# Second projection's operands prepared in two parts on VectorE, last norm factors stored by halves, second weight block rounded between decays

## The chip, the cores and the metric

The kernel runs on one core of one Trainium2 chip. The core has a matrix engine (TensorE, PE in the profile; its weight loads are PEld), VectorE (DVE), ScalarE (ACT), GpSimd (POOL) and SyncE (SP), which here only issues transfers. Each engine works through its own instructions in order and waits on semaphores for the others. Transfers between the chip's main memory (DRAM) and on-chip memory (SBUF) are issued by SP and by ScalarE. Matrix products gather in PSUM, which has eight banks of 128 x 512 values.

The metric is the device time of one execution in microseconds (us). The kernel before took 1428.77, 1432.49 and 1429.33 us in three runs, a median of 1429.33.

## The reference

One layer of a hybrid decoder on 1024 tokens of width 1024, in f32. The input is normed and modulated by a conditioning vector, projected once to all branches (`proj = h @ w_in`), and two branches are computed and merged:

```python
y_a = spatial_gating(gelu(gm_u), gelu(gm_v), ...) * silu(gm_z)
xbc = silu(causal_depthwise_conv(xbc, conv_w, conv_b))
xs, bm, cm = split(xbc, ...)                      # 2048, 8 x 128, 8 x 128
y_b = ssd_scan(xh, dt, a, bm, cm) + xh * d_skip   # 8 groups, chunks of 128 tokens
yz = (y_b * silu(ssm_z)).reshape(b, s, 8, 256)
y_b = rms_norm(yz, ssm_norm_w)                    # over the 256 channels of each group
merged = sigmoid(g_a) * (y_a @ w_proj_a) + sigmoid(g_b) * (y_b @ w_proj_b)
out = x + gate * (merged @ w_out)                 # then a final rms_norm over the width
```

`y_b` has 2048 channels, so `w_proj_b` is 2048 x 1024; `w_proj_a` and `w_out` are 1024 x 1024.

## The kernel before

Every large product is made of three products of 128 x 512 tiles: each operand is split into a high part (rounded by ScalarE, a cast) and a low part (the value less the high part, a subtraction on VectorE), and high x high, high x low and low x high are added in one PSUM bank.

The kernel runs in stages. First come the norm of the input and the input projection, each block of it as a scheme of seven half-size products p1 to p7 in place of eight. Then the scan: eight groups of 256 channels, each in four steps of 256 tokens (`front`, `back`, and `prep`, `decay` for the steps to come). Between the scan's steps TensorE is filled with the first projection, `y_a @ w_proj_a` (`proj_a`, a generator from which `draw(n)` takes n steps; PSUM tiles `pma`, result `tha`, stored to `mt_d`). Its weights come in eight blocks: `wa_load` loads one (`wa`), `wa_high` rounds it on ScalarE (`wah`), `wa_low` makes the low part on VectorE (`wal`). `decay_rows` and `decay_exps` make the scan's decay factors with exponentials on ScalarE (tiles `ea`, `dcy`) and a mask on GpSimd between them.

When a group's scan is through for half of the tokens (q is 0 or 1), `post` leaves its output `yz` in DRAM (`yb_d`) and, with a delay counted in slots of the program, squares it on ScalarE (`squares`), sums the squares over channels with TensorE (`post2`, bank `pq`) and reads the sums on VectorE (`post2b`, tile `ssq`). GpSimd raises them to the power -1/2, and `post3` turns them with a TensorE transpose into rows, copies those on VectorE (`cwt` for even groups, `tri` for odd ones) and stores them from ScalarE to `rs_d`. For groups 6 and 7 post3 is called in the second projection, into banks of p2 (`yp`), after the third and fourth unit of p1.

The second projection, `y_b @ w_proj_b`, follows, again by seven products, in the order p1, p2, p5, p3, p6, p7, p4. Each has eight k steps, so there are 56 units, of 12 matmuls of 128 x 512 each (`multiply`, L1548). A unit needs `loads(u)` on SP: the scan's output (`yn`), the norm factors of its group spread over all partitions (`rb`, one for two units, from `rs_d`), and the weights, which are raw for p1 and p2 (`p1r`, `p2r`, to be split) and split beforehand in DRAM for the others (`wb_d`). Then `operands(u)`: VectorE norms `yn` (`y_norm`), for some products forms a sum or difference of blocks, ScalarE rounds it (`bh`), VectorE makes the low part (`bl`), and for p1 and p2 ScalarE and VectorE split the weights in the same way (`p1a`, `p2a`). The tiles `bh` and `bl` have four places each, `rb` three, the weights nine.

The order is written out by hand in this stage: every instruction of VectorE, ScalarE and GpSimd is kept in program order. After each `multiply(u)` come `loads(u + 6)` and `operands(u + 4)` (`ahead`). After the last unit of a product `emptied_banks` frees its banks before `ahead`: ScalarE copies them (p1, p5, p3), or VectorE adds them to sums (`c<-c,yp` for p2, `p<-p,x` for p6 and p7). p2, p5 and p3 use four banks (`yp`), p1, p6, p7 and p4 the other four (`x`); a product that starts anew, as p5, waits until its bank is read. `merged` then multiplies a block by its gate and adds the other branch (tiles `tg`, `ma`, with the split `mmh`, `mml`), in odd units from p3 on. The output projection (`po`) and the final norm end the kernel.

Transfers complete on eight semaphores, which SP's and ScalarE's transfers take in turn, so that an issue waits for the transfer eight before it.

Of the kernel before, what the change touches and what calls it, by code (L numbers as in the profile page):

```python
# [35 lines left out]
def hybrid_kernel(  # L36
# [55 lines left out]
    def tp(dst, src, idn):  # L92
        pin(PE.transpose(dst, src, idn))  # L93
# [409 lines left out]
    def later(delay, f, *a):  # L503
        tasks.append((slot[0] + delay, f, a))
# [455 lines left out]
    class Group:  # L960
# [158 lines left out]
        def post(self, q):  # L1119

            g = self.g
            yz = self.yz[q]

            def leave():
                for j in range(2):
                    store(yb_d[2 * g + j][:, q * 512 : (q + 1) * 512], yz[:, j])

            if g < NG - 2 or q == 0:
                later(3, leave)
                later(9, self.squares, yz, [yz[:, j] for j in range(2)])  # L1130
                later(17, self.post2, q, yz[:, 0])
            else:
                later(1, leave)
                sq = [turn(r, f"sq{g}", F32) for r in ((y1_r, ym_r) if g < NG - 1 else (war_r[0], war_r[0]))]
                later(1, self.squares, yz, sq, pin)
                later(9, self.post2, q, sq[0])

        def squares(self, yz, sq, keep=lambda i: i):
# [11 lines left out]
        def post2b(self, q, pq):  # L1150
            g = self.g
            V.tensor_scalar(ssq[:, g * NCH + q * 4 : g * NCH + q * 4 + 4], pq[:, 0:4], 1.0 / 256, EPS,
                            op0=ALU.mult, op1=ALU.add)
            release(f"pq{g}_{q}")
            if q == 1:
                c8 = slice(g * NCH, (g + 1) * NCH)
                G.tensor_tensor(ssq[:, c8], ssq[:, c8], nhalf, op=ALU.pow)
                if g < NG - 2:
                    later(8, self.post3)

        def post3(self, at_once=False):

            g = self.g
            pr = rows_bank[0](f"pr{g}")
            tp(pr[0:NCH, 0:P], ssq[:, g * NCH : (g + 1) * NCH], ident)
            row = (cwt, tri)[g % 2][0:NCH, :]
            V.tensor_copy(row, pr[0:NCH, 0:P])
            release(f"pr{g}")
            to = rs_d[g].rearrange("o (c p) -> (o c) p", p=P)
            if at_once:  # L1170
                store(to, row)
            else:
                later(1, store, to, row)
# [171 lines left out]
    def proj_a():  # L1345

        for dd in range(KT):
# [8 lines left out]
            for k in range(KT):  # L1356
                wh, wl = was[dd][k // 4]
                yh, yl = yas[k]
                ks = slice(k % 4 * P, (k % 4 + 1) * P)
                for n, (lw, r) in enumerate(((wh, yh), (wh, yl), (wl, yh))):  # L1360
                    for h in range(2):
                        mm(pms[h], lw[:, ks], r[h], k + n == 0, k == KT - 1 and n == 2)
                    yield
                if k == 1 and dd + 1 < KT:
                    wa_high(dd + 1)
                if k == 3 and dd + 1 < KT:
                    wa_low(dd + 1)
            for h in range(2):
                V.scalar_tensor_tensor(ths[h], ths[h], 1.0, pms[h], op0=ALU.add, op1=ALU.mult)
# [10 lines left out]
    tha_r, ea_r, y1_r, ym_r = (ring(c) for c in (4, 3, 2, 2))  # L1380
    st_tag = room.pop(0)
    st_home = take("st_home", st_tag, F32)
    fetch(4)
    wa_load(1)
    fetch(5)
    while tasks:
# [5 lines left out]
    free.extend(BANKS)  # L1392
    for k in (6, 7):
        ya_operand(k)
    decays(4)
    fill = proj_a()

    left = [3 * KT * KT]
# [106 lines left out]
            n = k if nm == "p1" else KT + k  # L1505
            load(raw, w_proj_b[n * P : (n + 1) * P, 0:512])

    def operands(u):

        nm, k = units[u]  # L1510
        if nm in fresh:
            n, h = fresh[nm]
            y_norm(n + k, h)
        b11, b12 = yt[k, 0], yt.get((k, 1))
        b21, b22 = yt.get((KT + k, 0)), yt.get((KT + k, 1))
        t = {"p1": b11, "p2": b21, "p5": b12, "p3": b22, "p6": b12, "p7": b11, "p4": b21}[nm]
# [12 lines left out]
        if nm not in WB:  # L1529
            a, raw = aops[u], raws.pop(u)  # L1530
            keep(A.copy(a[:, 0], raw))
            keep(V.tensor_sub(a[:, 1], raw, f32(a[:, 0])))
        if nm == "p6":
            V.tensor_sub(b21, b21, b12)
# [83 lines left out]
    ya_free()  # L1618
    for tags in (war_r[0][0][:2], wah_r[0][0][2:], wal_r[0][0][2:], y1_r[0], ym_r[0], tha_r[0]):
# [44 lines left out]
    for u, (nm, k) in enumerate(units):  # L1664
# [153 lines left out]
```

## Time and profile before

| | us |
|---|---|
| median of three runs | 1429.33 |
| the profiled execution | 1429.86 |
| its span, first to last instruction | 1428.1 |
| TensorE busy | 1392.1 |
| VectorE busy | 1035.0 |
| ScalarE busy | 780.3 |
| GpSimd busy | 206.0 |
| second projection, from its first matmul to its last | 1161.0 to 1331.95 |

The mean granted clock of TensorE is 0.995 of full speed. The profile names an instruction by engine, line, operation and tiles: `p2bl<-yn,p2bh` writes the low part of a p2 operand from the normed output and its high part. Much of VectorE's and ScalarE's work passes through a helper and has its line, L56, so it is told apart by its tiles. A bracket at a row's end is the idle time of the engine just before it, and what ended that. "issue" as a releaser says that the profile shows nothing that the engine waited for. Busy time of a long row of matmuls runs a little over the space between their starts, since one matmul begins before the one ahead has ended.

### The profile page before, as it was taken

How to read it: one execution, taken by the hardware profiler on the slowest of the kernel's cores; microseconds unless marked ns; L12 is line 12 of the kernel's file. 1: busy time of each engine (PE TensorE's matmuls, PEld its weight loads, DVE VectorE, ACT ScalarE, POOL GpSimd, SP SyncE). 2: the span in 40 equal slices, each digit the busy share in tenths (PEclk: the TensorE clock that was granted, in tenths of full speed). 3: DMA queues.
4: the chain of work that ended last, by engine and by line, in shares of the span. 5: the costliest groups of instructions: out<-in, count | busy, mean ns of one | idle time of the engine just before them, and what ended most of it. 6: DMA issues, size and time to landing. Idle time of an engine off the chain costs nothing.

```text
span 1428.1 us, 20481 instructions
## 1 busy us (share of the span) xinstructions
PE 1392.1 (97%) x7087; PEld 1152.1 (81%) x7087; DVE 1035.0 (72%) x1827; ACT 780.3 (55%) x1438; POOL 206.0 (14%) x190
## 2 busy tenths in 40 slices
PE   8999999999999999999999999999999998999997
PEld 6688888888888888888887788878888876877886
DVE  5686676777667888788877885668878757677743
ACT  6664576566656665555665455667767523223401
POOL 0000000000000000000010100037878820000000
PEclk9999999999999999999999999999999999999999
DMA  9552333333332677586686764799779478976531
GB/s 281 147 162 89 119 118 104 104 103 113 109 110 90 206 225 225 176 261 208 184 252 195 221 189 141 243 325 307 276 260 324 163 261 300 332 245 215 186 118 74
DMA packets 260524, 277.08 MB, mean 194 GB/s; under 512 B 13596, under 2 KB 210628, under 8 KB 260420
## 3 DMA queue, kind: packets, MB, share of 16 engines
q1 hardware_dynamic: 179396, 195.37, 43.5%
q10 hardware_dynamic: 81024, 80.40, 16.2%
q8 instruction: 56, 0.92, 0.3%
q14 instruction: 48, 0.39, 0.1%
HBM read 191.40 MB, written 84.31 MB: 193 GB/s over the span
## 4 chain that ended last, share of the span: by engine, by line
PE 68%; DMA 11%; DVE 9%; ACT 5%; issue 3%; POOL 3%; SPq 1%; ACTq 0%; POOLq 0%; DVEq 0%
PE xuz L585 6%; PE xcb L585 6%; PE xx L585 5%; PE xz L585 5%; PE po L90 4%; PE xg L585 4%; PE yuz L585 3%; PE xv L585 3%; PE ycb L585 3%; PE yz L585 2%; PE yg L585 2%; PE yx L585 2%; PE pma L90 2%; PE yp L1548 2%; PE yv L585 2%
## 5 line engine op out<-in xcount | busy, mean ns | idle before, releaser
L796 POOL TENSOR_TENSOR wog<-wog,gb 128x1024 f32<-128x1024 f32 x8 | 22.4, 2796 | 725.8 <-DMA wbr<-in_w_proj_b_dram 569.4
L56 ACT ACTIVATE dcy<-dcy,nacs 128x128 f32<-128x128 f32 x256 | 78.4, 389 | 34.3 <-POOL dcy L56 18.2
L56 POOL TENSOR_SCALAR_AFFINE_SELECT dcy<-dcy 128x1024 f32<-128x1024 f32 x32 | 37.3, 1166 | 105.5 <-ACT ea L56 105.3
L908 ACT ACTIVATE ac<-ac 128x1024 f32<-128x1024 f32 x32 | 34.0, 1061 | 19.7 <-DVE ac L906 19.6
L90 PE MATMUL pma<-yh,wah 128*128 128x512 f32 x128 | 43.2, 419 | 0.1
L90 PE MATMUL pma<-yh,wal 128*128 128x512 f32 x128 | 42.8, 415 | 0.0
L56 DVE TENSOR_TENSOR ym<-yn,ea 128x512 f32<-128x512 f32 (+1 forms) x32 | 19.9, 623 | 29.3 <-PE yn L90 29.2
L56 POOL TENSOR_TENSOR yz<-y,sl 128x512 f32<-128x512 f32 x32 | 41.1, 1283 | 0.6
L56 ACT ACTIVATE ea<-dcy 64x512 f32<-64x512 f32 x64 | 40.3, 629 | 1.4 <-DMA dcy<-acs_d 1.0
L56 DVE TENSOR_TENSOR dcy<-dcy,pc 128x1024 f32<-128x1024 f32 x32 | 39.0, 1219 | 2.6 <-PE pc L93 1.4
L90 PE MATMUL pma<-yl,wah 128*128 128x512 f32 x128 | 40.0, 393 | 0.0
L1771 POOL TENSOR_TENSOR r<-r,fnw 128x256 f32<-128x256 f32 (+1 forms) x3 | 2.7, 915 | 250.6 <-ACT xr L1770 250.6
L56 POOL TENSOR_TENSOR y<-y,ym 128x512 f32<-128x512 f32 (+1 forms) x32 | 36.5, 1142 | 14.9 <-DVE ym L56 14.8
L906 DVE SCALAR_TENSOR_TENSOR ac<-c2x,cwt,ac 128x1023 f32<-128x1023 f32 (+2 forms) x24 | 31.8, 1325 | 9.0 <-ACT ac L904 7.1
L90 PE MATMUL yi<-dcy,xd 128*64 128x128 f32 x512 | 35.0, 279 | 0.9 <-DVE xe L56 0.6
L906 DVE SCALAR_TENSOR_TENSOR ac<-c2cb,cwt,ac 128x1023 f32<-128x1023 f32 (+2 forms) x24 | 30.6, 1276 | 7.1 <-ACT ac L904 7.0
L1781 ACT ACTIVATE xr<-r 128x1024 f32<-128x1024 f32 x7 | 7.4, 1061 | 51.1 <-issue 39.0
L90 PE MATMUL sp<-xe,bn 128*128 128x256 f32 x112 | 32.7, 409 | 0.0
L90 PEld LDWEIGHTS yi<-dcy,xd 128*64 128x64 f32 x512 | 27.3, 136 | 5.2 <-issue 2.7
L906 DVE SCALAR_TENSOR_TENSOR ac<-c1cb,cwt,ac 128x1023 f32<-128x1023 f32 (+2 forms) x24 | 30.7, 1279 | 0.7 <-ACT ac L904 0.7
L906 DVE SCALAR_TENSOR_TENSOR ac<-c1x,cwt,ac 128x1023 f32<-128x1023 f32 (+2 forms) x24 | 30.7, 1277 | 0.0
L56 DVE SCALAR_TENSOR_TENSOR y<-sl,dskt,yi 128x256 f32<-128x256 f32 x64 | 27.7, 473 | 4.0 <-POOL yz L56 2.8
(2842 smaller groups left out, 4379.1 us busy)
## 6 DMA issues: line engine op xcount, KB each, us to landing
sl<-s_d SPq DMA_DIRECT2D x32, 768.0 KB
s_d<-ac ACTq DMA_DIRECT2D x32, 512.0 KB
dcy<-acs_d SPq DMA_DIRECT2D x32, 512.0 KB
aw<-in_ada_w_dram SPq DMA_DIRECT2D x16, 512.0 KB
wbr<-in_w_proj_b_dram SPq DMA_DIRECT2D x64, 128.0 KB
wb_d<-wbb ACTq DMA_DIRECT2D x32, 256.0 KB
wb_d<-wbc ACTq DMA_DIRECT2D x32, 256.0 KB
yb_d<-yz ACTq DMA_DIRECT2D x32, 256.0 KB
```

What stands on the lines that cost most here:

```text
L56: return lambda *a, **k: tc.keep_in_program_order(f(*a, **k))
L90: pin(PE.matmul(acc, l, r, start=first, stop=last))
L585: pin(PE.matmul(ps, lw[:, k * P : (k + 1) * P], r[k], start=first and n + k == 0, stop=n == 2 and k == 3, skip_group_check=not first))
L796: G.tensor_mul(w, w, gb)
L906: V.scalar_tensor_tensor(ac[:, s:], cc[:, : S - s], conv_wt[:, 3 - s, i : i + 1], ac[:, s:], op0=ALU.mult, op1=ALU.add)
L908: A.activation(ac, ac, AF.Silu)
L1548: pin(PE.matmul(ps[j], a[:, v, js], r, start=first and n + k == 0, stop=n == 2 and k == KT - 1, skip_group_check=not first))
L1771: G.tensor_mul(r[:, cs], r[:, cs], fnw[:, cs])
L1781: A.activation(xr, r, AF.Square, accum_out=sq[:, 0:1])
```

## The change

Five things change.

1. `operands(u)` is cut in two. `ready(u)` holds the norm and the sums or differences of blocks; `operands(u)` rounds on ScalarE, calls `ready(u + 1)`, and then makes the low parts on VectorE.
2. Loads run seven units ahead instead of six. In the loop that ends the scan, the operands of the first four units are called ahead of `run_tasks` instead of behind it, `ready(0)` stands in the first round, and one more unit is loaded there.
3. For groups 6 and 7 the factors go by halves of the tokens: a power of 128 x 4 for each half instead of one of 128 x 8, and transposes, copies and stores of 4 rows, after units 0 and 1 of p1 (first halves) and 4 and 5 (second halves).
4. The last group's second half leaves, and is squared, three slots after its scan instead of one.
5. The second weight block of the first projection is loaded ahead of the fourth step's scan inputs, and rounded between the exponentials of the third step's decay, before the projection starts; within the projection only the blocks from the third on are rounded.

```diff
@@ Group.post
             else:
-                later(1, leave)
+                wait = 1 if g < NG - 1 else 3
+                later(wait, leave)
...
-                later(1, self.squares, yz, sq, pin)
+                later(wait, self.squares, yz, sq, pin)
@@ Group.post2b
-            if q == 1:
-                c8 = slice(g * NCH, (g + 1) * NCH)
-                G.tensor_tensor(ssq[:, c8], ssq[:, c8], nhalf, op=ALU.pow)
-                if g < NG - 2:
-                    later(8, self.post3)
-
-        def post3(self, at_once=False):
+            if g >= NG - 2:
+                self.roots(4 * q, 4)
+            elif q == 1:
+                self.roots(0, NCH)
+                later(8, self.post3, 0, NCH)
+
+        def roots(self, c0, n):
+            cs = slice(self.g * NCH + c0, self.g * NCH + c0 + n)
+            G.tensor_tensor(ssq[:, cs], ssq[:, cs], nhalf[:, 0:n], op=ALU.pow)
+
+        def post3(self, c0, n, at_once=False):
...
-            to = rs_d[g].rearrange("o (c p) -> (o c) p", p=P)
+            to = rs_d[g].rearrange("o (c p) -> (o c) p", p=P)[c0 : c0 + n]
@@ proj_a
-                if k == 1 and dd + 1 < KT:
+                if k == 1 and 0 < dd < KT - 1:
                     wa_high(dd + 1)
-                if k == 3 and dd + 1 < KT:
+                if k == 3 and 0 < dd < KT - 1:
                     wa_low(dd + 1)
@@ before the scan
-    fetch(4)
+    fetch(3)
     wa_load(1)
     fetch(5)
...
-    decays(4)
+    ahead = [(groups[g], i) for g, i in order[2:4]]
+    ahead[0][0].decay_rows(ahead[0][1])
+    wa_high(1)
+    ahead[0][0].decay_exps(ahead[0][1])
+    wa_low(1)
+    ahead[1][0].decay(ahead[1][1])
+    done_d[0] = 4
@@ second projection
-    def operands(u):
+    source = {}
+
+    def ready(u):
...
+    def operands(u):
+
+        nm, k = units[u]
+        t = source.pop(u)
         hi, lo = turn(bh_r, f"{nm}bh{k}"), turn(bl_r, f"{nm}bl{k}")
-        keep = pin if u < 4 else lambda i: i
-        keep(A.copy(hi, t))
-        keep(V.tensor_sub(lo, t, f32(hi)))
-        bops[u] = hi, lo
+        A.copy(hi, t)
         if nm not in WB:
             a, raw = aops[u], raws.pop(u)
-            keep(A.copy(a[:, 0], raw))
-            keep(V.tensor_sub(a[:, 1], raw, f32(a[:, 0])))
+            A.copy(a[:, 0], raw)
+        if u + 1 < len(units):
+            ready(u + 1)
+        V.tensor_sub(lo, t, f32(hi))
+        if nm not in WB:
+            V.tensor_sub(a[:, 1], raw, f32(a[:, 0]))
+        bops[u] = hi, lo
...
-    LEAD, LOAD = 4, 6
+    LEAD, LOAD = 4, 7
...
     while tasks:
+        n += 1
         draw(2)
+        ya_free()
+        if n == 1:
+            ready(0)
+        elif n in (2, 4, 6, 8):
+            operands(n // 2 - 1)
+        if n in (4, 5, 6, 7):
+            loads(n - 1)
         run_tasks()
-        ya_free()
-        n += 1
-        if n in (2, 4, 6, 8):
-            operands(n // 2 - 1)
-        if n in (4, 5, 6):
-            loads(n - 1)
...
         multiply(u, ps)
-        if nm == "p1" and k in (2, 3):
-            groups[NG - 4 + k].post3(True)
+        if nm == "p1" and k % 4 < 2:
+            groups[NG - 2 + k % 4].post3(k // 4 * 4, 4, True)
```

What this moves shows in the engines' orders at three places. On VectorE, where p5 begins, the rows before are the norm, subtraction and low part of the second and third p5 unit, the four adds that empty p2's banks, and the norm and subtraction of the fourth:

```order
L56 SCALAR_TENSOR_TENSOR yn_1_11721<-yn_1_11721,par_140,rb_1_11696 128x512
L56 TENSOR_TENSOR yn_1_11721<-yn_1_11721,yn_0_11249 128x512
L56 TENSOR_TENSOR p5bl_11775<-yn_1_11721,p5bh_11774 128x512
L56 SCALAR_TENSOR_TENSOR yn_1_11746<-yn_1_11746,par_140,rb_1_11744 128x512
L56 TENSOR_TENSOR yn_1_11746<-yn_1_11746,yn_0_11256 128x512
L56 TENSOR_TENSOR p5bl_11799<-yn_1_11746,p5bh_11798 128x512
L56 TENSOR_TENSOR c_0_11614<-c_0_11614,yp_11412 128x512
L56 TENSOR_TENSOR c_1_11616<-c_1_11616,yp_11413 128x512
L56 TENSOR_TENSOR c_2_11618<-c_2_11618,yp_11414 128x512
L56 TENSOR_TENSOR c_3_11620<-c_3_11620,yp_11415 128x512
L56 SCALAR_TENSOR_TENSOR yn_1_11768<-yn_1_11768,par_140,rb_1_11744 128x512
L56 TENSOR_TENSOR yn_1_11768<-yn_1_11768,yn_0_11311 128x512
```

Each low part (`p5bl`) stands right behind the subtraction that makes its value. In the changed kernel the same stretch of VectorE reads:

```order
L56 SCALAR_TENSOR_TENSOR yn_1_11736<-yn_1_11736,par_140,rb_1_11734 128x512
L56 TENSOR_TENSOR yn_1_11736<-yn_1_11736,yn_0_11251 128x512
L56 TENSOR_TENSOR p5bl_11789<-yn_1_11711,p5bh_11788 128x512
L56 SCALAR_TENSOR_TENSOR yn_1_11760<-yn_1_11760,par_140,rb_1_11734 128x512
L56 TENSOR_TENSOR yn_1_11760<-yn_1_11760,yn_0_11313 128x512
L56 TENSOR_TENSOR p5bl_11811<-yn_1_11736,p5bh_11810 128x512
L56 TENSOR_TENSOR c_0_11628<-c_0_11628,yp_11422 128x512
L56 TENSOR_TENSOR c_1_11630<-c_1_11630,yp_11423 128x512
L56 TENSOR_TENSOR c_2_11632<-c_2_11632,yp_11424 128x512
L56 TENSOR_TENSOR c_3_11634<-c_3_11634,yp_11425 128x512
L56 SCALAR_TENSOR_TENSOR yn_1_11784<-yn_1_11784,par_140,rb_1_11782 128x512
L56 TENSOR_TENSOR yn_1_11784<-yn_1_11784,yn_0_11324 128x512
```

The value of the next unit (`yn`) now stands ahead of the low part of a unit whose value was made one unit earlier (`p5bl_11811` takes `yn_1_11736`); the four adds keep their place behind the third p5 unit's low part, with the fourth unit's value ahead of them too.

On ScalarE, at the start of p1, the order before has the two stores of the first projection's last block (`mt_d_82`), the roundings of the fifth and sixth unit, and the stores of the factors of groups 6 and 7 (`rs_d_64`, `rs_d_65`) between the next ones:

```order
L56 DMA mt_d_82<-tha_0_11265 128x512
L56 DMA mt_d_82<-tha_1_11268 128x512
L56 CAST p1bh_11440<-yn_0_11327 128x512
L56 CAST p1a_11329<-p1r_11330 128x512
L56 CAST p1bh_11464<-yn_0_11349 128x512
L56 CAST p1a_11351<-p1r_11352 128x512
L56 DMA rs_d_64<-cwt 8x128
L56 CAST p1bh_11493<-yn_0_11434 128x512
L56 CAST p1a_11436<-p1r_11437 128x512
L56 DMA rs_d_65<-tri 8x128
L56 CAST p1bh_11520<-yn_0_11458 128x512
L56 CAST p1a_11460<-p1r_11461 128x512
```

In the changed kernel the first halves of these stores come two units earlier:

```order
L56 DMA mt_d_82<-tha_0_11260 128x512
L56 DMA mt_d_82<-tha_1_11263 128x512
L56 DMA rs_d_64<-cwt 4x128
L56 CAST p1bh_11450<-yn_0_11324 128x512
L56 CAST p1a_11326<-p1r_11327 128x512
L56 DMA rs_d_65<-tri 4x128
L56 CAST p1bh_11479<-yn_0_11345 128x512
L56 CAST p1a_11347<-p1r_11348 128x512
L56 CAST p1bh_11503<-yn_0_11363 128x512
L56 CAST p1a_11365<-p1r_11366 128x512
L56 CAST p1bh_11529<-yn_0_11445 128x512
L56 CAST p1a_11447<-p1r_11448 128x512
```

`rs_d_64` and `rs_d_65` of 4 rows stand ahead of the fifth and sixth rounding; the second halves, further down than these rows, stand ahead of the ninth and tenth.

On VectorE, where the scan starts (`y` and `st_home` are the first scan step's output and state), this piece of the difference shows the low part of the second weight block:

```order
-L56 SCALAR_TENSOR_TENSOR y_0_8708<-sl_0_8253,dskt,yi_0_8696 128x256 x2
-L56 COPY st_home<-sp_0_8705 128x256
-L56 TENSOR_TENSOR wal_0_8714<-wa_0_8619,wah_0_8713 128x512
-L56 TENSOR_TENSOR wal_1_8717<-wa_1_8621,wah_1_8716 128x512
+L56 TENSOR_TENSOR wal_0_8654<-wa_0_8614,wah_0_8653 128x512
+L56 TENSOR_TENSOR wal_1_8657<-wa_1_8616,wah_1_8656 128x512
+L56 SCALAR_TENSOR_TENSOR y_0_8716<-sl_0_8253,dskt,yi_0_8704 128x256 x2
+L56 COPY st_home<-sp_0_8713 128x256
```

It moved ahead of the first step's output.

More of the change, by code (lines that the diff above doesn't have):

```diff
@@ L1154, in post2b @@
             release(f"pq{g}_{q}")
-            if q == 1:
-                c8 = slice(g * NCH, (g + 1) * NCH)
-                G.tensor_tensor(ssq[:, c8], ssq[:, c8], nhalf, op=ALU.pow)
-                if g < NG - 2:
-                    later(8, self.post3)
-        def post3(self, at_once=False):
+            if g >= NG - 2:
[7 more added lines that the diff above has]
+        def post3(self, c0, n, at_once=False):
             g = self.g
             pr = rows_bank[0](f"pr{g}")
-            tp(pr[0:NCH, 0:P], ssq[:, g * NCH : (g + 1) * NCH], ident)
-            row = (cwt, tri)[g % 2][0:NCH, :]
-            V.tensor_copy(row, pr[0:NCH, 0:P])
+            tp(pr[0:n, 0:P], ssq[:, g * NCH + c0 : g * NCH + c0 + n], ident)
+            row = (cwt, tri)[g % 2][0:n, :]
+            V.tensor_copy(row, pr[0:n, 0:P])
             release(f"pr{g}")
-            to = rs_d[g].rearrange("o (c p) -> (o c) p", p=P)
+            to = rs_d[g].rearrange("o (c p) -> (o c) p", p=P)[c0 : c0 + n]
             if at_once:
@@ L1515, in operands @@
         b21, b22 = yt.get((KT + k, 0)), yt.get((KT + k, 1))
-        t = {"p1": b11, "p2": b21, "p5": b12, "p3": b22, "p6": b12, "p7": b11, "p4": b21}[nm]
+        source[u] = {"p1": b11, "p2": b21, "p5": b12, "p3": b22, "p6": b12, "p7": b11, "p4": b21}[nm]
         if nm == "p5":
@@ L1523, in operands @@
             V.tensor_sub(b11, b12, b11)
+    def operands(u):
+        nm, k = units[u]
+        t = source.pop(u)
         hi, lo = turn(bh_r, f"{nm}bh{k}"), turn(bl_r, f"{nm}bl{k}")
-        keep = pin if u < 4 else lambda i: i
-        keep(A.copy(hi, t))
-        keep(V.tensor_sub(lo, t, f32(hi)))
-        bops[u] = hi, lo
+        A.copy(hi, t)
         if nm not in WB:
             a, raw = aops[u], raws.pop(u)
-            keep(A.copy(a[:, 0], raw))
-            keep(V.tensor_sub(a[:, 1], raw, f32(a[:, 0])))
+            A.copy(a[:, 0], raw)
[5 more added lines that the diff above has]
+        bops[u] = hi, lo
         if nm == "p6":
-            V.tensor_sub(b21, b21, b12)
+            V.tensor_sub(yt[KT + k, 0], yt[KT + k, 0], t)
         elif nm == "p7":
```

## The prediction

> **What bounds the kernel now.** First the page's table of busy time.
>
> ```profile
> PE 1392.1 (97%) x7087; PEld 1152.1 (81%) x7087; DVE 1035.0 (72%) x1827; ACT 780.3 (55%) x1438; POOL 206.0 (14%) x190
> ```
>
> TensorE works 97% of the span of 1428.1 us, so a change can gain what TensorE stands idle, or runs at a low clock, and little else. Next its waits from 1155 us on, where the second projection lies (columns: total, times, longest), and then windows by product (length, busy us of PE, PEld, DVE, ACT and POOL, granted clock, DMA share, GB/s).
>
> ```profile
> PE yp L1548 <- issue: 6.4, 1, 6.4
> PE x L1548 <- issue: 3.4, 2, 2.8
> PE x L1548 <- ACT p6bh L56: 1.3, 1, 1.3
> PE x L1548 <- DVE ssq L56: 1.1, 1, 1.1
> ```
>
> ```profile
> 1161.00:1184.40 23.40, 22.30 (x99) 17.96 (x98) 16.06 (x30) 7.99 (x14) 3.72 (x2) 1.00 0.74 236
> 1184.40:1206.17 21.77, 21.77 (x97) 17.83 (x95) 15.37 (x24) 10.47 (x19) 0.00 (x0) 1.00 0.91 309
> 1206.17:1212.74 6.57, 0.16 (x2) 0.03 (x1) 4.98 (x9) 1.24 (x2) 0.00 (x0) 0.90 0.97 348
> 1212.74:1237.20 24.46, 24.46 (x96) 20.02 (x97) 16.65 (x25) 6.61 (x11) 0.00 (x0) 0.89 0.97 364
> 1237.20:1258.98 21.78, 21.78 (x98) 18.02 (x97) 13.63 (x21) 6.20 (x11) 0.00 (x0) 1.00 0.74 245
> 1258.98:1284.47 25.49, 23.97 (x97) 18.90 (x95) 17.96 (x29) 8.15 (x14) 0.00 (x0) 0.93 0.77 257
> 1284.47:1287.43 2.96, 0.15 (x1) 0.03 (x1) 2.20 (x5) 0.62 (x1) 0.00 (x0) 1.00 0.36 144
> 1287.43:1309.30 21.87, 21.87 (x96) 17.91 (x96) 15.89 (x26) 6.53 (x11) 0.00 (x0) 1.00 0.44 136
> 1309.30:1331.95 22.65, 22.09 (x98) 18.15 (x98) 18.15 (x31) 9.98 (x18) 0.00 (x0) 1.00 0.81 309
> 1212.74:1218.50 5.76, 5.76 (x14) 4.58 (x15) 4.93 (x8) 0.62 (x1) 0.00 (x0) 0.52 0.85 302
> 1271.30:1276.60 5.30, 5.07 (x14) 3.81 (x15) 3.78 (x6) 1.24 (x2) 0.00 (x0) 0.68 0.41 152
> 1220.00:1240.00 20.00, 20.00 (x90) 16.57 (x89) 12.33 (x19) 6.59 (x11) 0.00 (x0) 1.00 1.01 386
> ```
>
> The first nine rows are p1, p2, a gap, p5, p3, p6, a gap, p7, p4. An undisturbed product takes 21.77 us (p2), 2.72 for each of its eight units. The nine rows last 170.95 against 7 x 21.77 = 152.4: 18.6 us are lost here. The two gaps have no releaser of their own ("issue"). VectorE shows what ends them.
>
> ```profile
> 1199.50 0.69 DVE L56 TENSOR_TENSOR p2bl<-yn,p2bh 128x512 fp32r<-128x512 f32 x1 [0.76 <-ACT p2bh L56]
> 1200.11 0.68 DVE L56 TENSOR_TENSOR p2a<-p2r,p2a 128x512 fp32r<-128x512 f32 x1
> 1200.71 0.74 DVE L56 SCALAR_TENSOR_TENSOR yn<-yn,par,rb 128x512 f32<-128x512 f32 x1
> 1202.22 0.69 DVE L56 TENSOR_TENSOR p2bl<-yn,p2bh 128x512 fp32r<-128x512 f32 x1 [0.76 <-ACT p2bh L56]
> 1204.21 0.69 DVE L56 TENSOR_TENSOR yn<-yn,yn 128x512 f32<-128x512 f32 x1
> 1205.67 0.69 DVE L56 TENSOR_TENSOR p5bl<-yn,p5bh 128x512 fp32r<-128x512 f32 x1 [0.76 <-ACT p5bh L56]
> 1211.96 2.48 DVE L56 TENSOR_TENSOR c<-c,yp 128x512 f32<-128x512 f32 x4
> ```
>
> One unit's operands take VectorE 1202.22 - 1199.50 = 2.72 us, as long as TensorE's unit, and 0.76 of it is a wait for ScalarE's rounding of what VectorE has just normed. So VectorE never gains on TensorE: at 1206.17, when p2 ends, it has the first p5 unit ready, though its program puts the operands of three p5 units ahead of the four adds that empty p2's banks (c<-c,yp). They come at 1211.96, and p5, which needs those banks, starts at 1212.74.
>
> **The change part by part.** *Operands in two parts.* The norm (and the subtraction) of unit u+1 goes between ScalarE's rounding of unit u and VectorE's low part of it, so the 0.76 falls away where that work fills it: 2.72 - 0.76 = 1.96 a unit of p1 and p2. A p5 unit is norm 0.75, subtraction 0.69, low part 0.61 (1199.50 to 1200.11), 2.05. From the fifth unit on VectorE gains 2.72 - 1.96 = 0.76 a unit. The fifth unit's low part stands in this row:
>
> ```profile
> 1169.74 0.69 DVE L56 TENSOR_TENSOR p1bl<-yn,p1bh 128x512 fp32r<-128x512 f32 x1 [0.87 <-ACT p1bh L56]
> ```
>
> TensorE without its wait reaches that unit at 1161.0 + 4 x 2.72 = 1171.9, so it is in time even if nothing moves there; at worst (rival c below) at about 1171.5. Fourteen units later, unit 18, VectorE would be at 1171.5 + 10 x 1.96 + 4 x 2.05 = 1199.3. What then holds it is its ring of four operand slots: unit 18 takes the slot of unit 14, which TensorE leaves at 1161.8 + 15 x 2.72 = 1202.6. Rounding and low part (0.76 + 0.61) end at about 1204.0, the first bank's add 0.6 later, and TensorE wants that bank at 1205.3. Each further bank is wanted 0.68 later and added in 0.6. So the 6.57 should shrink to a step of 0.05 to 0.1, with a margin of some 0.7.
>
> With the gap goes what follows it. The row 1212.74:1218.50 has a granted clock of 0.52, and p5 lasts 24.46 instead of 21.77: 2.7. The Trainium skill, "TensorE: Matmul & The Clock Gate", section "What's actually happening", says that the clock halves after an idle window of about 3.4 us and recovers after as long a busy one; this gap agrees. But p6's wait of 1.3 is followed by a clock of 0.68 over 5.30 us, and p7, after an idle stretch of 2.8, shows 1.00, which does not agree. In p6 TensorE is busy 23.97 us for work of 21.77, 2.2 more, behind that short wait: by the page a leftover wait of 1 us costs 1, by p6's row up to 3.2. The sum below has no such wait, and the range goes by the row.
>
> *p6 and p7.* VectorE's merge steps stand in p3 and p6.
>
> ```profile
> 1267.14 0.68 DVE L56 SCALAR_TENSOR_TENSOR tg<-tg,c 128x512 f32<-128x512 f32 x1
> 1269.24 0.69 DVE L56 TENSOR_TENSOR mmh<-tg,mmh 128x512 fp32r<-128x512 f32 x1 [0.69 <-ACT mmh L56]
> 1269.85 0.68 DVE L56 TENSOR_TENSOR yn<-yn,yn 128x512 f32<-128x512 f32 x1
> 1271.29 0.69 DVE L56 TENSOR_TENSOR p6bl<-yn,p6bh 128x512 fp32r<-128x512 f32 x1 [0.76 <-ACT p6bh L56]
> 1286.65 2.47 DVE L56 TENSOR_TENSOR p<-p,x 128x512 f32<-128x512 f32 x4
> 1309.25 2.47 DVE L56 TENSOR_TENSOR p<-p,x 128x512 f32<-128x512 f32 x4
> ```
>
> One merge takes 1269.85 - 1267.14 = 2.71, its 0.69 of waiting kept. In p3's time VectorE then has four merges, four p3 units of 1.36 (0.75 + 0.61) and four p6 units of about 1.9 (three of 0.61 to 0.69): 10.8 + 5.4 + 7.6 = 23.8 against 21.8. It falls back 2.0 from a lead of about three units, 8 us, and regains it in p6. So p6bh and p6bl are ready in time: p6 loses 25.49 - 21.8 = 3.7, and the adds of 1286.65 come when their banks do: 2.9 of 2.96. Before p4 a merge stands ahead of the adds (1309.25) whatever the lead; of 22.65 - 21.9 = 0.7 I take half, 0.35 (bounds 0 and 0.7).
>
> *Halves of the norm factors.* TensorE gets two more transposes:
>
> ```profile
> L93 PE MATMUL yp<-ident,ssq 128*8 128x128 f32 x2 | 0.5, 271 | 0.0
> ```
>
> 0.27 each or less, 0.5 at most; 0.3 taken. p1's wait of 1.1 for ssq goes, as the second half's sums are read before p1 starts, with the operands' waits out of VectorE's way. p1: 1.1 - 0.3 = 0.8. The last group's squares run later on ScalarE, behind the first two units' roundings; TensorE's sums of them may then wait. No row shows it: between 0 and p1's present 1.1, the nearest wait for such sums. I take 0.5.
>
> The stores of the rows hold queues today:
>
> ```profile
> 1164.93 0.32 SPq L99 DMA_DIRECT2D rb<-rs_d  x1
> 1170.87 0.32 SPq L99 DMA_DIRECT2D yn<-yb_d  x1
> 1175.95 0.29 ACTq L56 DMA_DIRECT2D rs_d<-cwt  x1
> 1181.79 0.32 SPq L99 DMA_DIRECT2D rb<-rs_d  x1
> ```
>
> SP stands 5.8 from the store's issue at 1175.95 to the load of those factors at 1181.79. With the first half stored two units earlier, that load no longer waits. The new first halves stand ahead of the fifth and sixth rounding on ScalarE, the second halves ahead of the ninth and tenth; all four have the leads above. Nothing taken.
>
> *One unit more of loading ahead* costs nothing where slots are free. From p5 on, a unit's loads and gates are 256 KB of yn, 128 of factors, 512 of weights and 256 of gates, 1.18 MB per 2.72 us, or 434 GB/s; the row 1220:1240 shows 386 at a share of 1.01. Eight units then need 24.4 instead of 21.8, 2.6 behind, covered by seven units (19 us) loaded ahead.
>
> *Second weight block.*
>
> ```profile
> PE pc L90 <- DVE tha L56: 1.9, 1, 1.9
> 945.22 1.29 DVE L56 TENSOR_TENSOR wal<-wa,wah 128x512 fp32r<-128x512 f32 x2 [7.76 <-ACT wah L56]
> 948.07 1.32 DVE L56 SCALAR_TENSOR_TENSOR tha<-tha,pma 128x512 f32<-128x512 f32 x2 [0.44 <-DMA tha<-th_d]
> ```
>
> Its low part comes earlier on VectorE, but the step that TensorE waits 1.9 for had itself waited 0.44 for a transfer. Taken 0; bounds a loss of 1.3 (the subtraction in the wrong place) and a gain of 1.9.
>
> **Sum.** 0.8 (p1) + 6.5 (gap) + 2.7 (p5) + 3.7 (p6) + 2.9 (gap) + 0.35 (p4) = 16.95, less 0.5: 16.4. The profiled execution took 1429.86, so 1413.4; it lies 0.5 above the median of the runs, 1429.33, so 1413.0 as a median.
>
> **Rivals.** *a) The merges eat the lead.* If VectorE's fall of 2.0 in p3 meets a lead that the slots keep near nothing, p6's waits and the gap before p7 stay: 0.8 + 6.5 + 2.7 - 0.5 = 9.5, so 1419.8. For it speaks the 23.8 against 21.8, against it that a full ring is 8 us.
>
> *b) The transfers bound p5 and p3.* If the lead in loads is not built, p5 takes 24.4: 1413.0 + 2.6 = 1415.6. For it the share of 1.01, against it p3's share of 0.74 behind it.
>
> *c) Slower: the half stores hold ScalarE.* The issue of a store can stand until an earlier transfer has landed; 5.8 is the longest hold in these rows. The first store follows TensorE's first unit, 1161.0 + 2.7 = 1163.7; a hold of 5.8, the wait for rounding (0.76) and the two low parts (1.2) end at 1171.5, against the 1171.9 wanted. Beyond about 6.2 every us goes to TensorE, once for each pair of stores. The lead then falls away too, and the gap and p5's clock come back (9.2). At a hold of 10: 2 x 3.8 + 9.2 = 16.8, which eats the 16.4; there it decides, and at 12 it gives 1413.0 + 2 x 5.8 + 9.2 = 1434. Nothing in the rows holds that long.
>
> *d) Nothing happens,* because another thing paces VectorE at 2.72, such as SP, which stood 5.9 from 1164.93 to 1170.87: VectorE's wait would then be named for a transfer instead of ScalarE, the gap stays, about 1428.
>
> **How the numbers follow.** The main case 0.70, a) 0.12, b) 0.07, c) 0.07, d) 0.04. The main case's own range: 1410 (p4's whole 0.7, no loss of 0.5 and part of the 1.9 at the second weight block) to 1417 (a leftover wait of 1 with p6's price of 3.2, and a little more). The whole range takes in a) and b): 1409.5 to 1420. About 0.3%, 4.3 us, is what a measurement can tell here (the three runs lie 3.7 apart). Faster: the main case, a) and b), 0.89; same: d), 0.04; slower: c), 0.07.
>
> **What would show it.** VectorE's rows in p2 have no wait for p2bh and are about 1.96 apart until the ring holds them, then 2.72 with a wait named PE or ACT; c<-c,yp falls into p2's last microseconds as four adds 0.68 apart; p5 and p6 last 21.8 at clock 1.00; no "issue" row above 0.5; no ssq wait. A DMA named as releaser of yn in p5 would mean b); a ScalarE wait for a transfer before p1bh, c); p6bh among TensorE's waits, a). The forecast fails most simply if the margin of 0.7 before p5 is spent: then a gap stays before p5, p7 or p4.

## The result, and the profile after

The changed kernel took 1416.79 us (median of five runs, 1416.1 to 1417.7), the kernel before 1429.33 (median of five). The ratio is 0.9911, with a 95% interval of 0.9896 to 0.9925: 0.9% faster. The forecast was 1413.0, between 1409.5 and 1420.0; of the 16.4 us forecast, 12.5 came. The profiled execution took 1416.10, 13.8 less than that of before, with a span of 1414.4.

The windows by product of the changed kernel, from the first matmul of one product to that of the next (p1, p2, p5, p3, p6, p7, p4; columns as before):

```profile
1162.12:1188.08 25.96, 23.01 (x102) 17.92 (x101) 15.80 (x31) 7.66 (x15) 2.99 (x3) 1.00 0.81 277
1188.08:1209.84 21.76, 21.76 (x98) 18.02 (x97) 20.10 (x33) 10.31 (x19) 0.00 (x0) 1.00 0.97 365
1209.84:1231.60 21.76, 21.76 (x98) 18.02 (x97) 15.26 (x24) 6.64 (x11) 0.00 (x0) 1.00 1.03 391
1231.60:1253.36 21.76, 21.76 (x98) 18.02 (x97) 15.79 (x25) 7.59 (x15) 0.00 (x0) 1.00 0.74 251
1253.36:1275.12 21.76, 21.76 (x98) 18.02 (x97) 17.59 (x30) 6.88 (x13) 0.00 (x0) 1.00 0.85 284
1275.12:1297.05 21.93, 21.92 (x98) 17.86 (x96) 15.51 (x26) 6.54 (x11) 0.00 (x0) 1.00 0.64 225
1297.05:1318.91 21.86, 21.86 (x97) 18.10 (x97) 18.10 (x29) 10.07 (x18) 0.00 (x0) 1.00 0.73 264
```

Both gaps and both stretches of low clock are gone: six products last 21.76 to 21.93 from start to start. p1 went the other way. From its start to p2's it took 23.40 before and takes 25.96 now. The seven take 156.79 us instead of 170.95, 14.2 less, and p1 begins 1.1 later (1162.12 instead of 1161.00). TensorE's waits in the whole stage are these two, both in p1:

```profile
PE yp L93 <- DVE ssq L56: 1.5, 1, 1.5
PE x L1568 <- ACT p1a L56: 1.4, 1, 1.4
```

VectorE's rows in p2, and where p5 begins:

```profile
1193.44 0.69 DVE L56 TENSOR_TENSOR p2bl<-yn,p2bh 128x512 fp32r<-128x512 f32 x1
1195.31 0.69 DVE L56 TENSOR_TENSOR p2bl<-yn,p2bh 128x512 fp32r<-128x512 f32 x1
...
1205.29 0.69 DVE L56 TENSOR_TENSOR p5bl<-yn,p5bh 128x512 fp32r<-128x512 f32 x1 [0.64 <-ACT p5bh L56]
1208.01 0.69 DVE L56 TENSOR_TENSOR p5bl<-yn,p5bh 128x512 fp32r<-128x512 f32 x1 [0.64 <-ACT p5bh L56]
1208.62 2.48 DVE L56 TENSOR_TENSOR c<-c,yp 128x512 f32<-128x512 f32 x4
```

A p2 unit takes 1195.31 - 1193.44 = 1.87 without a wait, and later, with the four places of the ring full, 2.72, TensorE's pace. The adds start at 1208.62 and the first ends at about 1209.2; p5 starts at 1209.84. The margin is 0.6.

p1's two waits begin on VectorE and ScalarE. VectorE, in the microseconds ahead of p1 and in it:

```profile
1153.83 0.75 DVE L56 SCALAR_TENSOR_TENSOR yn<-yn,par,rb 128x512 f32<-128x512 f32 x1 [2.37 <-DMA yn<-yb_d]
...
1157.45 0.75 DVE L56 SCALAR_TENSOR_TENSOR yn<-yn,par,rb 128x512 f32<-128x512 f32 x1 [1.40 <-DMA yn<-yb_d]
...
1161.05 0.75 DVE L56 SCALAR_TENSOR_TENSOR yn<-yn,par,rb 128x512 f32<-128x512 f32 x1 [1.65 <-DMA yn<-yb_d]
...
1164.30 0.75 DVE L56 SCALAR_TENSOR_TENSOR yn<-yn,par,rb 128x512 f32<-128x512 f32 x1 [1.15 <-DMA yn<-yb_d]
...
1166.17 0.16 DVE L56 TENSOR_SCALAR ssq<-pq 128x4 f32<-128x4 f32 x1
...
1175.93 0.69 DVE L56 TENSOR_TENSOR p1bl<-yn,p1bh 128x512 fp32r<-128x512 f32 x1 [7.56 <-ACT p1bh L56]
```

The next unit's norm now stands ahead of everything that follows on VectorE, and it waits for its load, 6.6 us in four pieces. The reading of the last sums of squares (1166.17) stands behind the fourth, 4.05 after p1's start. The transpose behind p1's first unit waits for it:

```profile
1156.90 1.03 POOL L56 TENSOR_TENSOR ssq<-ssq,nhalf 128x4 f32<-128x4 f32 x1
...
1166.47 0.27 PE L93 MATMUL yp<-ident,ssq 128*4 128x128 f32 x1 [1.47 <-DVE ssq L56]
```

The four columns that it turns, group 6's first half, had been raised to their power by 1157.93, and the power of the sums read last was made only from 1166.41 to 1167.42. So it did not wait for values. What is left is the bank: the row goes into a bank of p2, and these held sums of the scan (`pq`) before, which VectorE has to read first. This is read from the kernel; no row of the profile names the bank.

VectorE then waits 7.56 for the fifth rounding on ScalarE:

```profile
1166.95 0.93 ACTq L56 DMA_DIRECT2D mt_d<-tha  x2
1174.90 0.28 ACTq L56 DMA_DIRECT2D rs_d<-cwt  x1
1175.28 0.62 ACT L56 CAST p1bh<-yn 128x512 fp32r<-128x512 f32 x1 [12.30 <-PE x L1568]
```

The first half store comes 7.0 us after ScalarE has issued the two stores of the first projection's last block, though its row was ready at 1167.7. The fifth rounding stands behind it, and TensorE waits 1.4 for that unit's weights. The trace also holds the semaphore on which each transfer completes, and the time of each of its sixteen marks. The half store's semaphore is that of the second of the two stores, eight transfers before it in the program's order. That store, issued at 1167.55, set its last mark at 1174.82, and the half store was issued at 1174.90. SP was held in the same way: its load of `p2r` at 1173.56 has the semaphore of the first of the two stores, whose last mark came at 1173.49. The profile's list of SP's waits names this one, and its chain has the first store with the time that it took to land:

```profile
SPq L99 <- DMA mt_d<-tha: 5.0, 1, 5.0
```

```profile
1166.95 6.54 DMA mt_d<-tha
```

### The profile page after: what moved, and what is told of

Read it like the earlier page. It is cut to its first block, busy times and chain, and to the rows that moved or that the text cites. A ratio compares the mean times of both kernels' runs of the same rounds, so it can differ in the third digit from the quotient of the medians.

```text
span 1414.4 us, 20499 instructions
## 1 busy us (share of the span) xinstructions
PE 1388.5 (98%) x7089; PEld 1151.3 (81%) x7089; DVE 1033.7 (73%) x1829; ACT 780.9 (55%) x1438; POOL 205.2 (15%) x192
## 3 DMA queue, kind: packets, MB, share of 16 engines
q10 hardware_dynamic: 81024, 80.40, 16.4%
## 4 chain that ended last, share of the span: by engine, by line
PE 82%; DMA 6%; DVE 4%; ACT 2%; issue 2%; POOL 1%; SPq 1%; ACTq 0%; POOLq 0%; DVEq 0%
PE xuz L585 6%; PE xcb L585 6%; PE po L90 6%; PE xx L585 6%; PE x L1568 5%; PE xz L585 5%; PE yp L1568 5%; PE xg L585 4%; PE pma L90 4%; PE yuz L585 3%; PE xv L585 3%; PE ycb L585 3%; PE yx L585 3%; PE yz L585 3%; PE yg L585 2%
```

## The experiments

The kernels ran in three groups, each on one chip with the kernel before, which took 1430.70, 1431.24 and 1428.72 us there. Single executions of one kernel lay up to 7 us apart (1414.6 to 1421.6), so differences below about 2 us are read from the profiles.

**The split alone.** The kernel before, with `operands` cut in two:

```diff
+    def ready(u):          # norm, sums and differences of blocks
...
+    def operands(u):       # as in the changed kernel
...
         n += 1
+        if n == 1:
+            ready(0)
         if n in (2, 4, 6, 8):
             operands(n // 2 - 1)
```

> The kernel before with the split of the operands alone (the next unit's norm between rounding and low part); loads six ahead, whole norm-factor rows after units 2 and 3, weight block and last squares as before. Theory A (the split alone frees p5, p6 and p7): the 6.4 us gap before p5, the 2.8 before p7, p6bh's wait and the low clock all go, the six products p2 to p4 last 21.8 each, p1 about 22 to 24, so 1413 to 1415. Rival B (the halves and the longer load lead are needed): SP's 5.8 us stand at the whole store keeps the operands late, part of the gap before p5 stays, 1418 to 1424.

It took 1413.83 us, a ratio of 0.9884 (0.9868 to 0.9900). Windows of its p1 and p2:

```profile
1162.52:1184.87 22.35, 22.35 (x99) 17.88 (x98) 15.88 (x30) 7.83 (x15) 5.21 (x2) 1.00 0.76 236
1184.87:1207.52 22.65, 21.92 (x97) 17.86 (x96) 19.88 (x32) 11.16 (x20) 0.00 (x0) 1.00 0.96 349
```

Theory A holds: the split frees p5, p6 and p7 by itself, and p1, without the other edits, takes 22.35. A wait of 0.7 before p5 is what is left. Here too the next unit's norm stands ahead, and VectorE reads the last sums 3.75 us after p1's start (1166.27 against 1162.52); but the whole rows ask for their banks two units later, and TensorE does not wait.

**All but the split.** The changed kernel with `ready(u)` called at the head of `operands(u)`:

```diff
     def operands(u):
 
+        ready(u)
         nm, k = units[u]
...
-        if u + 1 < len(units):
-            ready(u + 1)
...
-        if n == 1:
-            ready(0)
-        elif n in (2, 4, 6, 8):
+        if n in (2, 4, 6, 8):
```

> The changed kernel with each unit's norm and subtraction back ahead of its own rounding; all else changed. Theory A: VectorE again takes 2.72 us a unit of p1 and p2, the gap before p5 is back at 4 to 7 us with the low clock behind it, 1427 to 1432. Rival B: the earlier half stores and loads give VectorE a lead of their own, the gap stays under 3 us, 1418 to 1423.

It took 1431.22 us, a ratio of 1.0003 (0.9994 to 1.0011). TensorE's longest waits are those of the kernel before:

```profile
PE yp L1567 <- issue: 6.5, 1, 6.5
PE x L1567 <- issue: 3.4, 2, 2.8
...
PE x L1567 <- ACT p6bh L56: 1.3, 1, 1.3
```

Rival B falls: the half stores, the longer lead in loads, the later squares and the weight block bring no measurable gain without the split.

**Half stores later.** The changed kernel with the half rows after units 2, 3, 6 and 7:

```diff
-        if nm == "p1" and k % 4 < 2:
-            groups[NG - 2 + k % 4].post3(k // 4 * 4, 4, True)
+        if nm == "p1" and k % 4 > 1:
+            groups[NG - 4 + k % 4].post3(k // 4 * 4, 4, True)
```

> The changed kernel with the first half rows transposed and stored after units 2 and 3 of p1, the second after units 6 and 7 (instead of 0, 1, 4, 5). Theory C (the first half store holds ScalarE until the first projection's last block has landed, 7.2 us, and that and the early transposes cost p1 its two waits of 1.5 and 1.4): both waits go, p1 falls from 25.96 to 22.5 to 23.5, 1413.5 to 1415. Rival D (the transfers themselves, at a DMA share of 1.0 from 1155 to 1170 us, are late whatever the stores do): the waits move to other names, p1 stays above 25, 1416 to 1417.5.

It took 1418.55 us, a ratio of 0.9915 (0.9901 to 0.9930), above both ranges. Neither theory had it. The two waits went, and two others came:

```profile
PE yp L1568 <- DVE tri L56: 1.5, 1, 1.5
...
PE yp L1568 <- DVE cwt L56: 1.3, 1, 1.3
```

The last transposes were put into p2's banks right ahead of p2, and the copies that free these stood behind VectorE's operand work. The edit made a wait of its own, so this run does not tell C from D.

**The second weight block as before.** The changed kernel with the old order of loads, roundings and decays:

```diff
-    fetch(3)
+    fetch(4)
     wa_load(1)
...
+    decays(4)
...
-                if k == 1 and 0 < dd < KT - 1:
+                if k == 1 and dd + 1 < KT:
                     wa_high(dd + 1)
```

> The changed kernel with the second weight block of the first projection loaded and rounded as before. Theory: it is worth nothing, since the step TensorE waits for waits itself for the gate's transfer: 1416 to 1417.5, TensorE's wait for tha 1.9 instead of 2.6 with two smaller waits back. Rival: the move is worth what TensorE's wait was in the kernel before, so undoing it costs 1 to 2 us: 1418 to 1419.

It took 1415.57 us, a ratio of 0.9900 (0.9886 to 0.9913), against 0.9911 for the changed kernel: nothing that can be measured. Its time lies a little below the theory's range, and TensorE's wait for `tha` was 1.4 instead of the 1.9 expected. A fourth kernel, the split with the block's new place and nothing else, agrees.

> The kernel before with the split and with the second weight block's new place, nothing else changed. If that block's place is worth what the profiles so far show (TensorE reaches p1 at 1162.1 with it, at 1163.8 without, but at 1162.5 in the kernel with the split alone), between 0 and 1.5 us less than the split alone: 1412 to 1414. If it is worth nothing, 1413 to 1415.

It took 1415.63 us, a ratio of 0.9885 (0.9867 to 0.9903), against 0.9884 for the split alone. Its time lies above both ranges, on a chip where the kernel before took 0.5 more; the ratios are the same.

**The changed kernel again,** as a measure for the next runs on its chip.

> The changed kernel itself, beside the next ones on the same chip: 1416 to 1418, p1 about 26 us with TensorE's two waits for ssq and p1a.

It took 1418.63 us, a ratio of 0.9908 (0.9890 to 0.9926), somewhat above the range, with waits of 1.1 for ssq and 2.0 for p1a. This p1 took 27.8 instead of about 26, at a clock of 0.94:

```profile
1162.31:1190.12 27.81, 24.59 (x102) 19.08 (x100) 17.23 (x33) 9.09 (x17) 2.99 (x3) 0.94 0.84 273
```

**Whole rows.** The changed kernel with the factors of groups 6 and 7 raised and stored whole, after units 2 and 3:

```diff
-            if g >= NG - 2:
-                self.roots(4 * q, 4)
-            elif q == 1:
+            if q == 1:
                 self.roots(0, NCH)
-                later(8, self.post3, 0, NCH)
+                if g < NG - 2:
+                    later(8, self.post3, 0, NCH)
...
-        if nm == "p1" and k % 4 < 2:
-            groups[NG - 2 + k % 4].post3(k // 4 * 4, 4, True)
+        if nm == "p1" and k in (2, 3):
+            groups[NG - 4 + k].post3(0, NCH, True)
```

> The changed kernel with the norm factors of groups 6 and 7 stored whole after units 2 and 3, as before; the split, the longer load lead, the later squares and the second weight block stay. Theory E (the half stores after units 0 and 1 are what p1 lost: they stand ahead of the fifth rounding, the whole rows stand two roundings later, where the lead hides them): p1 falls from 26 to 22.5 to 23.5 and the time by 2 to 3.5 us, 1413 to 1415. Rival F (the later squares and the loads seven ahead are what made the sums and the first loads late): p1 stays above 25, 1416 to 1418.

It took 1412.50 us, a ratio of 0.9867 (0.9846 to 0.9889), the least of all and a little below Theory E's range. Its four executions (1410.8 to 1414.2) lie below all six of the changed kernel on the same chip (1414.6 to 1421.6). Its p1, and then VectorE's last reading of sums and ScalarE at the stores:

```profile
1160.88:1183.76 22.88, 22.35 (x99) 17.96 (x98) 17.11 (x32) 8.83 (x16) 3.29 (x2) 1.00 0.87 309
```

```profile
1164.90 0.15 DVE L56 TENSOR_SCALAR ssq<-pq 128x4 f32<-128x4 f32 x1
...
1165.67 0.96 ACTq L56 DMA_DIRECT2D mt_d<-tha  x2
...
1168.29 0.62 ACT L56 CAST p1a<-p1r 128x512 fp32r<-128x512 f32 x1
1172.19 0.32 ACTq L56 DMA_DIRECT2D rs_d<-cwt  x1
1172.60 0.62 ACT L56 CAST p1bh<-yn 128x512 fp32r<-128x512 f32 x1 [3.69 <-DMA p2r<-in_w_proj_b_dram]
...
1177.75 0.28 ACTq L56 DMA_DIRECT2D rs_d<-tri  x1
```

Theory E holds, for both waits. The store still comes 5.6 us after the two of the last block, and the next one another 5.6 later, but two roundings stand ahead of it, so the fifth and sixth units are ready and TensorE does not wait for ScalarE. VectorE reads the last sums as late as in the changed kernel, 4.02 us after p1's start (4.05 there), but no row asks for that bank behind p1's first unit. A wait of 0.5 for `ssq` is left, at the third bank of p1's first unit.

**The last block's stores behind the half rows.** In the changed kernel, the stores of the first projection's last block wait until the first two half rows are out:

```diff
+    held = []
...
                 else:
-                    store(to, ths[h])
+                    held.append((to, ths[h]))
...
+        if u == 1:
+            for a in held:
+                store(*a)
```

> The changed kernel with the first projection's last block stored behind the first two half rows instead of ahead of them. Theory G (the half store stood 7.0 us on ScalarE because it had to wait for the stores of that block, just issued): the store goes out within 2 us, the fifth rounding comes by 1170, TensorE's wait of 1.4 for p1a goes, the wait of 1.5 for ssq stays: 1415 to 1416.5, p1 about 24.5. Rival H (any transfer issued then stands, since all transfers are late from 1155 to 1173): the store stands as long, p1 stays about 26, 1416 to 1418.

It took 1413.65 us, a ratio of 0.9876 (0.9857 to 0.9895), below both ranges. The half store goes out half a microsecond after its row is copied:

```profile
1166.35 0.27 ACTq L56 DMA_DIRECT2D rs_d<-cwt  x1
1166.71 0.62 ACT L56 CAST p1bh<-yn 128x512 fp32r<-128x512 f32 x1 [6.16 <-DVE yn L56]
...
1170.66 0.25 ACTq L56 DMA_DIRECT2D rs_d<-tri  x1
1171.24 0.83 ACTq L56 DMA_DIRECT2D mt_d<-tha  x2
```

TensorE's wait for p1a is gone, that for ssq is there (1.8), and p1 takes 24.24. Theory G holds: it was a store just issued that the half store waited for. Rival H has a small part in it, for the wait is for whatever transfer stands eight before. The first half store now shares its semaphore with a load of `p1r` from 1159.80, whose last mark came at 1166.27, and goes out 0.08 later; the second, whose row was copied by 1168.84, still stands until 1170.66, for a load of `yn` from 1165.00 with its last mark at 1170.59. These transfers are older, so the stand is short and TensorE does not wait for ScalarE.

**The adds made late.** To the kernel with whole rows, four and then eleven VectorE instructions of 0.6 us are added ahead of the adds that empty p2's banks; they change no value:

```diff
             elif nm == "p2":
+                for i in range(4 if j == 0 else 0):        # 11 in the second kernel
+                    V.tensor_tensor(more[i % 4][2], more[i % 4][2], more[i % 4][2], op=ALU.max)
                 V.tensor_add(more[j][2], more[j][2], psy[j])
```

> The kernel with the split and whole rows, with four more VectorE instructions of 0.6 us (the greater of a block and itself, which changes nothing) ahead of the four adds that empty p2's banks: these come 2.4 us later. Theory (the adds decide when p5 starts, with a margin of 0.6 us): a gap of 1.8 us before p5 and nothing more than 0.3 elsewhere if the clock stays, so p2's start to p5's 23.6 instead of 21.8; with the low clock that followed p6's wait of 1.3 in the kernel before, p5 lasts 24 instead of 21.8. Rival (another thing, such as a transfer, started p5): no gap.

> The same with eleven such instructions, 6.6 us. Theory: a gap of 6.0 us before p5 and the low clock behind it, p5 24.4 instead of 21.8, together 8.6 more than the kernel with whole rows, as in the kernel before. If the low clock there had another cause, p5 lasts 21.8.

They took 1418.58 and 1421.66 us (two executions each), ratios of 0.9924 (0.9902 to 0.9946) and 0.9946 (0.9926 to 0.9966). Windows of the gap, of the stretch behind it and of the rest of p5, first with four, then with eleven:

```profile
1206.57:1208.54 1.97, 0.16 (x1) 0.03 (x1) 1.97 (x5) 0.62 (x1) 0.00 (x0) 1.00 1.04 397
1208.54:1212.20 3.66, 3.66 (x10) 2.88 (x11) 3.63 (x7) 0.00 (x0) 0.00 (x0) 0.62 1.03 397
1212.20:1232.04 19.84, 19.84 (x88) 16.38 (x86) 12.25 (x19) 6.01 (x10) 0.00 (x0) 0.98 0.95 337
```

```profile
1206.85:1213.04 6.19, 0.16 (x1) 0.03 (x1) 6.19 (x12) 0.62 (x1) 0.00 (x0) 0.91 1.01 393
1213.04:1218.80 5.76, 5.76 (x14) 4.50 (x15) 5.01 (x8) 0.22 (x1) 0.00 (x0) 0.50 0.05 20
1218.80:1237.60 18.80, 18.80 (x84) 15.54 (x83) 10.87 (x16) 5.79 (x10) 0.00 (x0) 1.00 0.98 348
```

The adds decide when p5 starts: 2.4 late made 1.8 of waiting, 6.6 made 6.0 (the rows' 1.97 and 6.19 begin with the last matmul's slot), which is a margin of 0.6 each time. p5 then lasted 3.66 + 19.84 = 23.50 and 5.76 + 18.80 = 24.56 instead of 21.76. So lateness of 2.4 cost 3.7 in all, and of 6.6 9.0, much as in the kernel before. The medians, of two executions each, lie 6.2 and 9.3 above that of whole rows with loads six ahead (1412.39, below) on the same chip. The low clock can be placed more closely than in these windows. It is 0.50 for 3.41 us, from 0.87 us after p5's start with four instructions added:

```profile
1209.41:1212.82 3.41, 3.41 (x10) 2.66 (x9) 3.38 (x6) 0.00 (x0) 0.00 (x0) 0.50 0.96 375
```

Half of 3.41 is 1.7, which is what p5 lost (23.50 - 21.76 = 1.74). The kernel before behind p6's wait (1272.90 to 1276.31) and the changed kernel's repeat in p1 (1177.98 to 1181.39) show such a stretch of 3.41 at 0.50 too.

**The last squares at once.** The kernel with whole rows, with `wait = 1` for all groups.

```diff
-                wait = 1 if g < NG - 1 else 3
+                wait = 1
```

> The kernel with the split and whole rows, with the last group's second half left and squared one slot after its scan, as in the kernel before, instead of three. If the delay matters for p1 (it lets ScalarE round the first unit ahead of the squares, but makes the sums later): p1 differs from 22.9 by 0.5 to 1.5 us, either way; if not, 1411 to 1414.

It took 1414.78 us, a ratio of 0.9895 (0.9879 to 0.9912), and p1 25.92 instead of 22.88, which is 3.0 more where up to 1.5 was expected.

```profile
PE x L1567 <- DVE ssq L56: 2.1, 1, 2.1
...
PE x L1567 <- ACT p1a L56: 0.8, 1, 0.8
```

```profile
1150.76 3.21 ACTq L56 DMA_DIRECT2D yb_d<-yz  x2
1154.01 1.15 ACT L56 ACTIVATE sq<-yz 128x512 f32<-128x512 f32 x2 [7.89 <-DMA p1r<-in_w_proj_b_dram]
1155.66 2.12 ACTq L56 DMA_DIRECT2D mt_d<-tha  x2
```

ScalarE's issue of the last scan stores took 3.2 us, with loads in flight; the squares, two more stores (2.1) and only then the first unit's two roundings stood behind it, and VectorE waited 5.95 for the first. With the delay of three slots those are done ahead. In this frame the later squares help p1, where I had only a possible loss for them.

**Loads six ahead.** The kernel with whole rows, with `LOAD = 6` and one load fewer in the scan's last loop.

```diff
-    LEAD, LOAD = 4, 7
+    LEAD, LOAD = 4, 6
...
-        if n in (4, 5, 6, 7):
+        if n in (4, 5, 6):
             loads(n - 1)
```

> The kernel with the split and whole rows, with loads six units ahead instead of seven. Theory (the loads are covered either way, as the weights' nine places and the factors' three hold SP back): within 1 us of the kernel with whole rows, 1411.5 to 1414. Rival (the lead in loads covers p5's need of 434 GB/s): VectorE waits for yn in p5 or p3, 1 to 3 us more, 1414 to 1416.

It took 1412.39 us, a ratio of 0.9883 (0.9862 to 0.9903). p5 and p3 again lasted 21.76, and p1 23.40 with a wait of 0.6 for p1a: the seventh unit of lead in loads is not needed.

## Why the prediction was right, and where it was not

- *The gap before p5 (6.5), p5's clock (2.7), p6 (3.7), the gap before p7 (2.9).* Right in place and size, and shown by the split alone and by all but the split. The margin before p5, forecast at 0.7, is 0.6, shown by making the adds late. That late adds make the gap before p7 too was not tested in this way; it went with the split.
- *p4 (0.35 of 0.7).* All of the 0.7 came: p7 and p4 together took 43.79 instead of 44.52.
- *p1 (a gain of 0.8, less 0.5).* This step failed. p1 lost 2.6 instead of gaining 0.3, 2.9 us. The other products gave 0.6 more than forecast, so the stage gained 14.2 instead of 16.4; what else lies between that and the medians' 12.5 is within the scatter of the runs (TensorE reached p1 anywhere from 1160.0 to 1164.2 us in these kernels). Three terms were mis-sized.
  - "p1's wait of 1.1 for ssq goes, as the second half's sums are read before p1 starts" was wrong: the norms brought ahead waited 6.6 for their loads, and the last sums were read 4.05 after p1's start. That alone costs little, since with whole rows they were read 4.02 after it and TensorE waited 0.5. The half rows made it 1.5, as their first transpose asks for that bank behind p1's first unit.
  - The half stores, for which "nothing" was taken, cost 1.4: the first one was held for 7.0 us, where 5.8 was taken as the longest hold and 6.2 as the point from which TensorE pays. The 5.8 was that of a load on SP behind the whole row's store. Counting eight transfers back from the half store leads to a store just issued. This is rival c on a small scale, at a hold of 7 instead of 10, and paid once and not for each pair; the lead did not fall away.
  - The 0.5 for the later squares was not lost: TensorE waited for no squares in the changed kernel, and 0.2 in its repeat. In the kernel with whole rows the later squares gained 3.0 in p1.
- *The change as a whole.* The split alone has a ratio of 0.9884, the five edits together 0.9911 and 0.9908. So the other four bring nothing that these runs can tell, and the half rows among them cost p1 its two waits.
- *The second weight block (0, between -1.3 and 1.9).* Right: neither undoing nor adding it moved the time beyond the intervals. TensorE's wait for `tha` was between 1.4 and 3.8 in these kernels, with the block in either place.
- *One unit more of loading (0).* Right, by the run with six.
- *Rivals.* a) did not come: p6 has no wait, so the merges did not eat the lead. b) did not come, though the DMA share in p5 was 1.03. d) fell with the 1.87 a unit.
- *The price of a short wait.* The low clock was priced by p6's row, at 2.2. The added lateness of 2.4 bore out that a short wait can bring it, at 1.74 behind an idle time of 2.0. The Trainium skill, "TensorE: Matmul & The Clock Gate", section "What's actually happening", gives an idle window of about 3.4 us for it; the 2.0 does not agree with that. The prediction also counted p7's clock of 1.00 behind 2.8 of idling against that window, wrongly: 2.8 is shorter, so it fits.

What stays open: why the second of the last block's stores took 7.3 us to land in the changed kernel (1167.55 to 1174.82), and 3.2 in the kernel before (1168.24 to 1171.42). Why a short idle time brings the low clock at one place and not at another is open too. And whether p1 could lose its last us (22.88 against 21.76) was not tried.

## What to carry to other kernels

Where two engines hand work to each other in turn, look for a unit's time on the one that equals the time of the engine fed: it has no lead, and any burst of other work on it opens a gap. Putting the next unit's independent part into the wait gives the lead; but that part must have its input by then, or it holds up everything behind it in order. A small store placed ahead of urgent work on the issuing engine can stand for as long as a large one issued before it takes to land. Which one it is can be counted where the completion semaphores go round, here eight transfers back, over both issuing engines. So put the small store behind the work that feeds the bound. And a row that moves earlier needs more than its values early: the bank it is written to must be free by then.

## What the runs showed of the hardware that was not expected

- An idle time of 2.0 us on TensorE was followed by 3.66 us at a granted clock of 0.62, one of 6.2 by 5.76 at 0.50; two waits of 1.5 and 1.4 in the changed kernel's p1 were followed by none below 1.00, and in the repeat, waits of 1.1 and 2.0 came with a p1 at 0.94. A gap of 3.0 before p7, in the kernel before, had none either. So the price of a short gap is its length, or its length and about 1.7 us, half of a stretch of 3.41 at 0.50.
- A store of 2 KB stood 7.0 us behind two stores of 256 KB on the same issuing engine, and went out within half a microsecond of its row when those were issued after it. The semaphore that it takes is that of the transfer eight before it, and it was issued 0.08 us after that transfer's last mark, in both kernels.
